# Differential attention in an encoder layer: the first map's row sums kept as a factor, each head's norm issued beside the next head, the first q projected during cross attention

## The chip, the cores and the metric

One core of a Trainium2 chip runs the whole kernel. The metric is the device time in microseconds (us) of one execution, of which the median over several runs is taken. All times below are in us unless marked ns.

## The reference, cut to what matters

The kernel computes one layer of an encoder with three branches (a state-space branch "S5", differential attention, and cross attention to a memory), merges the branches through gates, and adds a feed-forward part. Two sequences of 512 tokens, 1024 wide, are done together. Only the differential attention and the cross attention are touched here:

```python
def _rmsnorm(x, g):
    return x * rsqrt(mean(x * x, axis=-1) + EPS) * g          # EPS = 1e-6

def _diff_attention(q, k, v, lam, subln_g, lambda_init):      # 4 heads, 2 maps of width 64 each, values 128 wide
    s = einsum('bqhd,bkhd->bhqk', q, k) * 64 ** -0.5
    probs = softmax(s, axis=-1).reshape(..., 4, 2, Q_BLOCK, L)
    w = probs[:, :, 0] - lam * probs[:, :, 1]
    o = einsum('bhqk,bkhe->bqhe', w, v)
    return _rmsnorm(o, subln_g) * (1.0 - lambda_init)         # over the 128 values of a head

def _cross_attention(q, mk, mv):                              # 4 heads of width 128, 256 memory rows
    probs = softmax(einsum('blhd,bmhd->bhlm', q, mk) * 128 ** -0.5)
    return einsum('bhlm,bmhd->blhd', probs, mv)
```

Before attention, q and k of differential attention are rotated in their first 16 of 64 columns. Gates are columns of the same input projection; the kernel takes them through tanh and stores them until the merge.

## The kernel before, in words

**Number format.** Everything is float32. A product of matrices is made on TensorE in three passes: each operand is split into a high part (float32r) and a low part, and high times high, low times high and high times low are added up in one PSUM bank. `split` (lines 106 to 113) makes the parts: a copy on ScalarE for the high part (109), a subtraction on VectorE for the low part (110). `weight` (115) loads a block of weights, 128x1024, into `wf` and splits it into `wh` and `wl`. `mm3` (124) issues the three passes of one step (129, 130, 132), and `proj` (134) makes one projection of 128 output columns: for each of the two sequences a bank `bkmm`, 8 steps of three matmuls, 512 columns each. A projection is so 48 matmuls.

**Order of the work.** The kernel is written with the Tile framework. It has a scheduler that simulates a timeline (line 1265) and puts the instructions of each engine in an order of its own: an instruction that is traced later may be moved ahead, as far as data and buffers allow. Each engine then runs its own instructions strictly in that order and waits at each for what it needs from the others. `tc.issue_after(x)` (in `behind`, 302) keeps what is traced inside it from being put ahead of instruction x. Buffers are taken from pools in turn; in the stage of interest the eight PSUM banks are divided into mm=2 (projections), sc=3 (scores), tr=2 (transposes and small results) and oo=1 (the product with the values); line 413.

**Cross attention** (447 to 482). For each of four heads one projection makes q of both sequences, which is split. Then for each sequence four tiles of 128 queries: scores against 256 memory rows in three matmuls (463 to 465) into a bank `bksc`, `softmax_parts` (363: the negated row maximum on VectorE, 366; its scaling, 368; exp with the row sums on ScalarE, 371; the reciprocal of the sums, 373), the scaling of the exps by it (467), two transposes (470) into `bktr`, and their split into `xpTh` and `xpTl`. After the four tiles six matmuls with the values (476 to 478) into `bkoo`, a copy to `osb` (480) and a store (481). In the last head's loop the values of differential attention for its first two heads are projected (`v_half`, 426 to 445), and one gate.

**Differential attention** (593 to 618). For each head h: `qk_tile` (496) projects q for both sequences (both maps, 64 rows each), rotates it with a product and a shuffle on VectorE (503, 505), a product and a sum on POOL (506, 507), and scales it into a tile for each map (510, 511); then the same for k, where copies on ScalarE (514), subtractions on VectorE (516) and four small DMAs in each sequence (515, 517) lay out high and low parts. The two mm banks of a projection come free when 503 and 505 have read them. Gates, the second half of the values and, in head 3, parts of the merge (575) are traced between (lists `NG_D`, `NM`, `VPOS`, lines 38 to 40).

Then `attend(h, s, ...)` (520) for each sequence s. For each of four tiles of 128 queries: the scores of both maps (533, 534; two matmuls of 512 columns each), `softmax_parts` for each map, the second map's reciprocal times -lam (537), the first map's exps times its reciprocal (538), the combination e1 * r1 + e0 (539), four transposes (542), and a split into the quarter's half of `pH` and `pL`. After each two tiles, twelve matmuls of 256 columns with the values (546 to 548). When all four tiles are through, the norm over the head's 128 values: `oo` is copied to `osb` (550), transposed by four transposes (554), squared on ScalarE with the sums in `ss` (557), and `factor` (166) makes the root (Sqrt on ScalarE, 169), its reciprocal (170) and, by four transposes of the broadcast column (173), a bank `bc` that holds the factor in every row. One product (559) applies factor and weights to `osb`, which goes to DRAM (560); the merge reads it later.

ScalarE holds one table of functions at a time. Exp (371) and Sqrt (169) are in different ones, so each norm brings a table load before the Sqrt and one before the next Exp; the trace shows them as `ACT_TABLE_LOAD` at the line of the instruction that needs the table.

For the prediction, head and sequence of an `attend` are written as two digits, its tiles as 0 to 3 and its maps as a and b: "scores 3b" is the second map of the fourth tile, T(0) the four transposes of a tile 0, "0a" of the next half the first map of the tile after. "pH(1)" is the copy for tile 1.

Of the kernel before, what the change touches and what calls it, by code (L numbers as in the profile page):

```python
# [10 lines left out]
F32 = mybir.dt.float32  # L11
F32R = mybir.dt.float32r
I32 = mybir.dt.int32
AF = mybir.ActivationFunctionType
# [5 lines left out]
P = 128  # L20
L = 512
# [27 lines left out]
def encoder(ctx: ExitStack, tc: tile.TileContext, a, out):  # L49
# [113 lines left out]
            PE.matmul(ss[:, t : t + 1], acc[:, t * P : (t + 1) * P], onec[:, 0:1], start=(t == 0), stop=(t == nt - 1))  # L163
        return factor(ss, n, nt)

    def factor(ss, n, nt=4):

        rs = rp.tile([P, 4], F32, tag="rs", name="rs", bufs=4)
        S.activation(out=rs[:, :nt], in_=ss[:, :nt], func=AF.Sqrt, scale=1.0 / n, bias=epsc)
        V.reciprocal(rs[:, :nt], rs[:, :nt])  # L170
        bc = aux()
        for t in range(nt):
            PE.transpose(bc[:, t * P : (t + 1) * P], rs[:, t : t + 1].broadcast_to([P, P]), ident)
        return rs, bc
# [127 lines left out]
    def behind():  # L302

        return tc.issue_after(last_mm.ins)
# [55 lines left out]
        nc.sync.dma_start(bD[0, t], sg)  # L360
    phase.close()

    def softmax_parts(pool, col, sc, n, scale, nm):

        nb = col.tile([P, 1], F32, tag=nm + "nb", name="nb")
        V.tensor_reduce(out=nb, in_=sc, axis=AX.X, op=ALU.max, negate=True)
        if scale != 1.0:
            V.tensor_scalar_mul(nb, nb, scale)
        e = pool.tile([P, n], F32, tag=nm + "e", name="e")
        sm = col.tile([P, 1], F32, tag=nm + "s", name="sm")  # L370
        S.activation(out=e, in_=sc, func=AF.Exp, bias=nb, scale=scale, accum_out=sm)
        r = col.tile([P, 1], F32, tag=nm + "r", name="r")
        V.reciprocal(r, sm)
        return e, r
# [72 lines left out]
    for h in range(4):  # L447
# [6 lines left out]
        for s in range(NS):  # L454
            if 2 * h + s == VPOS[0]:
                vv = v_half(0)
            ms = slice(s * NMEM, (s + 1) * NMEM)
            pTh = slot("xT", [P, 2, L], F32R, "xpTh")
            pTl = slot("xT", [P, 2, L], F32R, "xpTl")
# [33 lines left out]

    LO, HI = slice(0, 64), slice(64, P)

    def qk_tile(mt, is_q):
        o = proj(a["w_in"][mt], xh, xl)
        m0, m1 = (slot("qk", [P, NT], F32R, n_) for n_ in ("m0", "m1"))
        kl = (None, None) if is_q else tuple(slot("qk", [P, NT], F32R, n_) for n_ in ("l0", "l1"))
        for s in range(NS):  # L500
# [16 lines left out]
                    nc.sync.dma_start(l_[other, cs].bitcast(F32), l_[own, cs].bitcast(F32))  # L517
        return (m0, m1) if is_q else (m0, m1, *kl)

    def attend(h, s, q, kk, v):  # L520
        cs = slice(s * L, (s + 1) * L)
        oo = bank("oo")
        vs = slice((h % 2) * P, (h % 2) * P + P)
        vh, vl = v
        for qh in range(2):
            pH = slot("pT", [P, 4, 2 * P], F32R, "pH")
            pL = slot("pT", [P, 4, 2 * P], F32R, "pL")
            for q2 in range(2):
                q0 = s * L + (2 * qh + q2) * P
                er = []  # L530
                for mp in range(2):
                    sc = bank("sc")
                    PE.matmul(sc, q[mp][:, q0 : q0 + P], kk[mp][:, cs], start=True, stop=False)  # L533
                    PE.matmul(sc, q[mp][:, q0 : q0 + P], kk[2 + mp][:, cs], start=False, stop=True)  # L534
                    er.append(softmax_parts(ap_, acol, sc, L, 1.0, f"d{mp}"))
                (e0, r0), (e1, r1) = er
                V.tensor_tensor(out=r1, in0=r1, in1=nlam, op=ALU.mult)
                V.tensor_scalar_mul(e0, e0, r0)
                V.scalar_tensor_tensor(out=e0, in0=e1, scalar=r1, in1=e0, op0=ALU.mult, op1=ALU.add)
                tr = aux()  # L540
                for j in range(4):
                    PE.transpose(tr[:, j * P : (j + 1) * P], e0[:, j * P : (j + 1) * P], ident)
                split(pH[:, :, q2 * P : (q2 + 1) * P], pL[:, :, q2 * P : (q2 + 1) * P], tr.rearrange("p (j q) -> p j q", j=4))
            od = oo[:, qh * 2 * P : (qh + 1) * 2 * P]
            for j in range(4):
                PE.matmul(od, vh[:, j, vs], pH[:, j, :], start=(j == 0), stop=False)
                PE.matmul(od, vh[:, j, vs], pL[:, j, :], start=False, stop=False)
                PE.matmul(od, vl[:, j, vs], pH[:, j, :], start=False, stop=(j == 3))
        osb = rp.tile([P, L], F32, tag="nsq", name="osb", bufs=2)
        S.copy(osb, oo)  # L550
        tr = aux()
        ss = rp.tile([P, 4], F32, tag="ss", name="ss", bufs=3)
        for t in range(4):
            PE.transpose(tr[:, t * P : (t + 1) * P], osb[:, t * P : (t + 1) * P], ident)
        sq = new_acc()
        for t in range(4):
            S.activation(out=sq[:, t * P : (t + 1) * P], in_=tr[:, t * P : (t + 1) * P], func=AF.Square, accum_out=ss[:, t : t + 1])
        _, bc = factor(ss, P)
        V.scalar_tensor_tensor(out=osb, in0=osb, scalar=g04, in1=bc, op0=ALU.mult, op1=ALU.mult)
        nc.sync.dma_start(bD[1, h, :, cs], osb)  # L560


    mg = [None] * KD
# [31 lines left out]
    for h in range(4):  # L595
        if h == 2:
            vv = v1 or v_half(1)
        q = qk_tile(4 + h, True)
        if h < 3:
            gates(NG_D[h][0])  # L600
        kk = qk_tile(8 + h, False)
# [13 lines left out]
        if h < 3:  # L615
            gates(NG_D[h][3])
        else:
            merge(0, b0, range(NM[2], KD), first=True)
    b2 = merge_in(2)
    merge(2, b2, range(KD))  # L620
    phase.close()
# [647 lines left out]
```

## Time and profile before

| what | value |
|---|---|
| median of 3 runs | 1674.23 us (1672.43 to 1677.33) |
| the profiled execution | 1674.95 us |
| its span, first to last instruction | 1673.2 us |
| mean granted clock of TensorE | 0.989 of full speed |
| bytes moved by DMA | 197.69 MB, 118 GB/s in the mean |
| first to last store of a norm's result (560) | 605.4 to 823.3 us of the span |
| first to last scores of cross attention start (463) | 422.4 to 523.4 us |

The profiled execution is one run of the kernel, recorded by the hardware. Its engines are PE (TensorE, matmuls), PEld (TensorE loading weights, which overlaps PE), DVE (VectorE), ACT (ScalarE), POOL (GpSimd) and SP (SyncE, whose queue issues the DMAs). An engine's busy share is the time in which it ran instructions; the idle time ahead of an instruction is put down to what ended it. A row of the view by stretches gives a window, then for each engine its busy time and, in brackets, its instructions, then the granted clock (1.00 is full speed), the mean busy share of the DMA engines and GB/s. A row of the timeline gives an instruction's start, its length, its engine, its line, out<-in and its shape, and in square brackets the time that its engine had been idle before it and what ended that. A row of the groups gives line, engine, operation, out<-in, count, then busy time and mean ns of one, then the idle time before the group's instructions and what ended it. Matmul records overlap: the next one starts before the record of the last one ends.

### The profile page before, as it was taken

The numbers are of one execution on the slowest core, as the hardware profiler recorded it, in microseconds if no ns is written. First come the engines' busy times: TensorE is split into PE (matmuls) and PEld (weight loads), VectorE is DVE, ScalarE is ACT, GpSimd is POOL, SyncE is SP. The second block draws the span as 40 slices with busy tenths as digits, with TensorE's granted clock in tenths as the row PEclk, the third lists the DMA queues.
The fourth block names the chain that finished last, engine by engine and source line by source line (L and its number), as shares of the span: only waits on it lengthen the run. The fifth ranks groups of instructions, "written<-read, shape, count | busy, mean of one in ns | idle before, by whom it ended". The sixth has DMA issues, their size and how long they took to land.

```text
span 1673.2 us, 21052 instructions
## 1 busy us (share of the span) xinstructions
PE 1625.6 (97%) x7916; PEld 1357.8 (81%) x7916; DVE 1076.2 (64%) x1788; ACT 622.1 (37%) x1092; POOL 391.7 (23%) x253
## 2 busy tenths in 40 slices
PE   5999999999999999999999999999999999999997
PEld 4788887888897788878888878888888888888887
DVE  7946898154554776777655668777777777743324
ACT  6534412245343456554323443223323223421121
POOL 0001000000001121120243346555554552500021
PEclk9999999999999999999999999999999999999999
DMA  9343252747111221333554432322222223741302
GB/s 367 114 154 127 96 170 89 222 174 241 46 57 64 88 57 40 112 107 120 182 187 127 140 101 79 125 87 82 83 86 79 88 79 115 252 133 52 84 17 101
DMA packets 79269, 197.69 MB, mean 118 GB/s; under 512 B 11072, under 2 KB 26688, under 8 KB 79168
## 3 DMA queue, kind: packets, MB, share of 16 engines
q1 hardware_dynamic: 79168, 196.35, 35.4%
q8 instruction: 62, 1.02, 0.3%
q14 instruction: 39, 0.32, 0.1%
HBM read 141.82 MB, written 50.30 MB: 115 GB/s over the span
## 4 chain that ended last, share of the span: by engine, by line
PE 79%; DVE 11%; DMA 3%; issue 2%; ACT 2%; POOL 1%; SPq 1%; DVEq 0%; POOLq 0%; ACTq 0%
PE bkmm L129 15%; PE bkmm L132 15%; PE bkmm L130 15%; PE bkmm L738 8%; PE bkmm L737 8%; PE bkmm L739 8%; DVE st L1140 1%; DVE wl L110 1%; PE bktr L1122 1%; POOL mg L587 1%; PE bksc L533 1%; DMA c_n<-cD 1%; PE bksc L534 1%; PE bkmm L438 1%; PE bkmm L439 1%
## 5 line engine op out<-in xcount | busy, mean ns | idle before, releaser
L109 ACT CAST wh<-wf 128x1024 fp32r<-128x1024 f32 (+4 forms) x164 | 142.3, 868 | 385.4 <-PE bkmm L130 225.9
L132 PE MATMUL bkmm<-xh,wl 128*128 128x512 f32 x640 | 252.1, 394 | 3.0 <-DVE wl L110 3.0
L129 PE MATMUL bkmm<-xh,wh 128*128 128x512 f32 x640 | 251.8, 393 | 2.3 <-DVE t L505 1.2
L130 PE MATMUL bkmm<-xl,wh 128*128 128x512 f32 x640 | 251.7, 393 | 0.0
L738 PE MATMUL bkmm<-tl,wh 128*128 128x512 f32 x612 | 240.1, 392 | 2.5 <-DVE tl L110 2.5
L737 PE MATMUL bkmm<-th,wh 128*128 128x512 f32 x612 | 239.9, 392 | 0.0
L739 PE MATMUL bkmm<-th,wl 128*128 128x512 f32 x612 | 238.5, 391 | 0.0
L110 DVE TENSOR_TENSOR wl<-wf,wh 128x1024 fp32r<-128x1024 f32 (+4 forms) x164 | 175.7, 1072 | 94.5 <-ACT wh L109 93.9
L129 PE MATMUL bkmm<-ah,wh 128*128 128x512 f32 (+1 forms) x408 | 147.1, 361 | 0.2 <-ACT wh L109 0.2
L130 PE MATMUL bkmm<-al,wh 128*128 128x512 f32 (+1 forms) x408 | 147.0, 360 | 0.0
L132 PEld LDWEIGHTS bkmm<-xh,wl 128*128 128x128 f32 x640 | 120.7, 189 | 29.1 <-DVE wl L110 3.8
L129 PEld LDWEIGHTS bkmm<-xh,wh 128*128 128x128 f32 x640 | 120.7, 189 | 28.7 <-DVE t L505 2.6
L130 PEld LDWEIGHTS bkmm<-xl,wh 128*128 128x128 f32 x640 | 120.5, 188 | 24.7 <-issue 0.4
L506 POOL TENSOR_TENSOR t<-t,rs 128x512 f32<-128x512 f32 x16 | 24.6, 1537 | 494.5 <-DVE t L505 494.5
L738 PEld LDWEIGHTS bkmm<-tl,wh 128*128 128x128 f32 x612 | 115.8, 189 | 28.1 <-DVE tl L110 4.2
L737 PEld LDWEIGHTS bkmm<-th,wh 128*128 128x128 f32 x612 | 115.8, 189 | 24.4 <-ACT th L109 0.3
L739 PEld LDWEIGHTS bkmm<-th,wl 128*128 128x128 f32 x612 | 115.5, 189 | 24.0
L132 PE MATMUL bkmm<-ah,wl 128*128 128x512 f32 (+1 forms) x408 | 127.4, 360 | 0.5 <-DVE wl L110 0.4
L802 POOL TENSOR_TENSOR up<-up,acc 128x512 f32<-128x512 f32 x44 | 85.1, 1957 | 149.4 <-DVE up L778 149.4
L862 DVE TENSOR_TENSOR y<-y,bkmm 128x512 f32<-128x512 f32 (+1 forms) x56 | 32.6, 608 | 111.4 <-PE bkmm L132 111.4
L153 POOL TENSOR_TENSOR acc<-acc,nsq 128x512 f32<-128x512 f32 (+1 forms) x32 | 38.0, 1187 | 241.2 <-ACT nsq L152 241.1
L132 PEld LDWEIGHTS bkmm<-ah,wl 128*128 128x128 f32 x408 | 76.9, 189 | 12.7 <-DVE wl L110 1.3
(585 smaller groups left out, 3272.3 us busy)
## 6 DMA issues: line engine op xcount, KB each, us to landing
wf<-in_w_in SPq DMA_DIRECT2D x40, 512.0 KB, 3.8
gD<-gt SPq DMA_DIRECT2D x24, 512.0 KB, 2.8
gl<-gD SPq DMA_DIRECT2D x24, 512.0 KB, 3.9
wf<-in_w_fg SPq DMA_DIRECT2D x22, 512.0 KB, 3.7
wf<-in_w_fu SPq DMA_DIRECT2D x22, 512.0 KB, 3.7
aD<-ac SPq DMA_DIRECT2D x22, 512.0 KB, 2.6
fl<-aD SPq DMA_DIRECT2D x22, 512.0 KB, 4.5
wf<-in_w_fo SPq DMA_DIRECT2D x16, 448.0 KB, 3.3
```

The costliest lines, as they stand in the source:

```text
L109: S.copy(hi, src)
L110: V.tensor_tensor(out=lo, in0=src, in1=hi.bitcast(F32), op=ALU.subtract)
L129: PE.matmul(outs[s], wh[:, ws], xh, start=(k == 0), stop=False)
L130: PE.matmul(outs[s], wh[:, ws], xl, start=False, stop=False)
L132: last_mm = PE.matmul(outs[s], wl[:, ws], xh, start=False, stop=(k == nk - 1))
L153: eng.tensor_tensor(out=acc[:, :n], in0=acc[:, :n], in1=sq[:, :n], op=ALU.add)
L506: PO.tensor_tensor(out=t2, in0=t2, in1=rope[1], op=ALU.mult)
L737: PE.matmul(ps, wh[:, ws_], th[:, o], start=(k == 0), stop=False)
L738: PE.matmul(ps, wh[:, ws_], tl[:, o], start=False, stop=False)
L739: PE.matmul(ps, wl[:, ws_], th[:, o], start=False, stop=(k == 3))
L802: PO.tensor_tensor(out=up, in0=up, in1=accs[s], op=ALU.mult)
L862: V.tensor_tensor(out=y[m][:, c : c + n], in0=y[m][:, c : c + n], in1=o_, op=ALU.add)
```

## The change

It has three parts, all between the last cross-attention head and the last differential head.

1. *The first map's row sums stay as a factor.* The map was e0/s0 - lam * e1/s1. Now it is e0 - lam * (s0/s1) * e1, which is s0 times as much for each query. For the first map `softmax_parts` takes a column of a 128x4 tile `s0` for its sums and leaves out the reciprocal; the scaling of the exps (538) goes; the small product (537) takes s0 as one more factor. The norm divides the factor out again: the mean of squares is s0 squared times as large, so the norm's epsilon must be multiplied by s0 squared. Two small operations on 128x4 make EPS * 128 * s0 * s0 and add it to the sums of squares, and the Sqrt has no bias of its own (`factor` gets an argument for it).
2. *The norm is issued beside the next head.* After the squares, `attend` no longer traces the factor, the product and the store, but puts them as a function into a list. The next `attend` calls it after its first half's value product, with `issue_after` that product's last matmul. The last norm is called after the head loop, behind the last projection matmul traced until then.
3. *The first q of differential attention is projected in cross attention.* Its `proj` is traced at the start of the last (head, sequence) pair of cross attention, and `qk_tile` of head 0 gets the two banks.

```diff
-    def factor(ss, n, nt=4):
+    def factor(ss, n, nt=4, bias=epsc):
...
-        S.activation(out=rs[:, :nt], in_=ss[:, :nt], func=AF.Sqrt, scale=1.0 / n, bias=epsc)
+        S.activation(out=rs[:, :nt], in_=ss[:, :nt], func=AF.Sqrt, scale=1.0 / n, bias=bias)
...
-    def softmax_parts(pool, col, sc, n, scale, nm):
+    def softmax_parts(pool, col, sc, n, scale, nm, sums=None):
...
-        sm = col.tile([P, 1], F32, tag=nm + "s", name="sm")
+        sm = col.tile([P, 1], F32, tag=nm + "s", name="sm") if sums is None else sums
         S.activation(out=e, in_=sc, func=AF.Exp, bias=nb, scale=scale, accum_out=sm)
+        if sums is not None:
+            return e, sm
         r = col.tile([P, 1], F32, tag=nm + "r", name="r")
         V.reciprocal(r, sm)
         return e, r
...
                 vv = v_half(0)
+            if 2 * h + s == 7:
+                q0 = proj(a["w_in"][4], xh, xl)
             ms = slice(s * NMEM, (s + 1) * NMEM)
...
-    def qk_tile(mt, is_q):
-        o = proj(a["w_in"][mt], xh, xl)
+    def qk_tile(mt, is_q, o=None):
+        o = o or proj(a["w_in"][mt], xh, xl)
...
+    norms = []
+
     def attend(h, s, q, kk, v):
...
+        s0 = acol.tile([P, 4], F32, tag="s0", name="s0", bufs=3)
         for qh in range(2):
...
             for q2 in range(2):
-                q0 = s * L + (2 * qh + q2) * P
+                qt = 2 * qh + q2
+                q0 = s * L + qt * P
...
-                    er.append(softmax_parts(ap_, acol, sc, L, 1.0, f"d{mp}"))
-                (e0, r0), (e1, r1) = er
-                V.tensor_tensor(out=r1, in0=r1, in1=nlam, op=ALU.mult)
-                V.tensor_scalar_mul(e0, e0, r0)
+                    er.append(softmax_parts(ap_, acol, sc, L, 1.0, f"d{mp}", None if mp else s0[:, qt : qt + 1]))
+                (e0, sm0), (e1, r1) = er
+                V.scalar_tensor_tensor(out=r1, in0=r1, scalar=nlam, in1=sm0, op0=ALU.mult, op1=ALU.mult)
                 V.scalar_tensor_tensor(out=e0, in0=e1, scalar=r1, in1=e0, op0=ALU.mult, op1=ALU.add)
...
-                PE.matmul(od, vl[:, j, vs], pH[:, j, :], start=False, stop=(j == 3))
+                pv = PE.matmul(od, vl[:, j, vs], pH[:, j, :], start=False, stop=(j == 3))
+            if qh == 0 and norms:
+                with tc.issue_after(pv.ins):
+                    norms.pop()()
...
-        _, bc = factor(ss, P)
-        V.scalar_tensor_tensor(out=osb, in0=osb, scalar=g04, in1=bc, op0=ALU.mult, op1=ALU.mult)
-        nc.sync.dma_start(bD[1, h, :, cs], osb)
+        V.scalar_tensor_tensor(out=s0, in0=s0, scalar=EPS * P, in1=s0, op0=ALU.mult, op1=ALU.mult)
+        V.tensor_tensor(out=ss, in0=ss, in1=s0, op=ALU.add)
+
+        def norm():
+            _, bc = factor(ss, P, bias=0.0)
+            V.scalar_tensor_tensor(out=osb, in0=osb, scalar=g04, in1=bc, op0=ALU.mult, op1=ALU.mult)
+            nc.sync.dma_start(bD[1, h, :, cs], osb)
+
+        norms.append(norm)
...
-        q = qk_tile(4 + h, True)
+        q = qk_tile(4 + h, True, None if h else q0)
...
             merge(0, b0, range(NM[2], KD), first=True)
+    with behind():
+        norms.pop()()
     b2 = merge_in(2)
```

## Prediction

> **What bounds the kernel now.** I read the page first: the share of each engine and the chain that ended last.
>
> ```profile
> span 1673.2 us, 21052 instructions
> PE 1625.6 (97%) x7916; PEld 1357.8 (81%) x7916; DVE 1076.2 (64%) x1788; ACT 622.1 (37%) x1092; POOL 391.7 (23%) x253
> PE 79%; DVE 11%; DMA 3%; issue 2%; ACT 2%; POOL 1%; SPq 1%; DVEq 0%; POOLq 0%; ACTq 0%
> ```
>
> TensorE (PE) is the bound. The change removes no matmul and no transpose (the built order of both kernels holds the same 7,679 TensorE rows; it differs only from the last cross-attention head to the last differential head), so it can only win or lose waits of PE. Next, busy time by stretches of 20 us. After the times come PE, PEld, DVE, ACT, POOL, the granted clock and DMA.
>
> ```profile
> 520.00:540.00 20.00, 18.12 (x84) 14.45 (x83) 7.68 (x22) 5.77 (x15) 2.59 (x2) 1.00 0.23 80
> 540.00:560.00 20.00, 17.93 (x76) 13.69 (x75) 10.38 (x17) 5.38 (x8) 8.60 (x6) 1.00 0.21 59
> 600.00:620.00 20.00, 18.98 (x125) 16.80 (x124) 16.26 (x33) 11.62 (x24) 5.39 (x4) 1.00 0.31 86
> 620.00:640.00 20.00, 19.76 (x156) 18.98 (x155) 11.80 (x28) 11.71 (x29) 0.00 (x0) 1.00 0.07 21
> 640.00:660.00 20.00, 17.70 (x105) 14.42 (x104) 14.83 (x38) 11.17 (x31) 0.00 (x0) 1.00 0.17 53
> 740.00:760.00 20.00, 16.56 (x77) 11.92 (x76) 19.45 (x35) 14.79 (x31) 4.26 (x2) 1.00 0.71 204
> ```
>
> PE idles in four places: the end of cross attention (1.88 + 2.07 us), the step from head 0 to 1 (1.02), head 1 (0.24 + 2.30) and the start of head 3 (3.44). Its steps, from timeline rows (start, length):
>
> ```profile
> 485.50 0.28 PE L438 MATMUL bkmm<-wh,xh 128*128 128x256 f32 x1
> 485.62 0.28 PE L463 MATMUL bksc<-mkvh,qh 128*128 128x256 f32 x1
> 524.89 0.60 PE L470 MATMUL bktr<-ident,e 128*128 128x128 f32 x4
> 525.24 0.48 PE L129 MATMUL bkmm<-xh,wh 128*128 128x512 f32 x1
> 525.56 0.39 PE L130 MATMUL bkmm<-xl,wh 128*128 128x512 f32 x1
> 525.79 0.39 PE L132 MATMUL bkmm<-xh,wl 128*128 128x512 f32 x1
> ```
>
> A matmul takes 0.12 us at 256 columns and 0.23 at 512, four transposes 0.35. A record lasts 0.39 but the next starts after 0.23, so each break loses 0.16 more than the idle column shows. With 5, 3, 6 and 6 breaks there, the places lose 4.75, 1.5, 3.5 and 4.4 us: 14.2 in all, the most that this change could win.
>
> Durations of the other engines, from the groups between 500 and 860 us (busy, mean ns):
>
> ```profile
> L366 DVE TENSOR_REDUCE nb<-bksc 128x1 f32<-128x512 f32 (+1 forms) x72 | 46.1, 652 | 19.1 <-PE bksc L534 11.8 <-PE bksc L465 7.1
> L110 DVE TENSOR_TENSOR pL<-bktr,pH 128x512 fp32r<-128x512 f32 x32 | 21.8, 681 | 1.7 <-ACT pH L109 1.7
> L538 DVE TENSOR_SCALAR e<-e,r 128x512 f32<-128x512 f32 x32 | 16.0, 503 | 0.6
> L373 DVE RECIPROCAL r<-sm 128x1 f32<-128x1 f32 x72 | 10.9, 156 | 13.8 <-ACT e L371 13.6
> L170 DVE RECIPROCAL rs<-rs 128x4 f32<-128x4 f32 x8 | 1.4, 178 | 10.2 <-ACT rs L169 10.2
> L110 DVE TENSOR_TENSOR xpTl<-bktr,xpTh 128x256 fp32r<-128x256 f32 x8 | 3.2, 417 | 6.4 <-ACT xpTh L109 6.4
> L467 DVE TENSOR_SCALAR e<-e,r 128x256 f32<-128x256 f32 x8 | 2.8, 350 | 0.2
> L371 ACT ACTIVATE e<-bksc,nb 128x512 f32<-128x512 f32 (+1 forms) x72 | 48.2, 670 | 24.4 <-DVE nb L366 21.4 <-DVE r L373 1.6 <-DVE nb L368 0.9
> L109 ACT CAST pH<-bktr 128x512 fp32r<-128x512 f32 x32 | 18.7, 585 | 29.6 <-PE bktr L542 29.3
> L109 ACT CAST vh<-bkmm 128x256 fp32r<-128x256 f32 x12 | 4.3, 380 | 4.5 <-PE bkmm L440 3.9 <-DVE vl L110 0.5
> L169 ACT ACT_TABLE_LOAD x8 | 10.3, 1283 | 0.1
> ```
>
> **The change, part by part.**
>
> *Row sums as a factor.* VectorE (DVE) loses 32 scalings (16.0 us) and 32 reciprocals (32 x 0.156 = 5.0). The 32 products with nlam stay one instruction. It gains 16 operations on 128x4; the trace has none of this kind, the nearest row is the reciprocal on 128x4 at 0.178, so 2.8 us (2.5 by the 128x1 reciprocal's 0.156, 10.4 if each took a full tile's 0.65). Net about -18 us of DVE, between -10.6 and -18.5. DVE is not the bound, and the chain from the second exp to the transposes (reciprocal, product, L539) keeps its length. So I count nothing by itself. In 740 to 760, where DVE is 97% busy, two scalings (1 us) would be felt; that is in the last place below. If DVE's slack elsewhere were gone, the same would count for each tile, in our favour.
>
> *Norms beside the next head.* Eight norms keep their work: four squares, a load of the Sqrt table, Sqrt, reciprocal, four transposes, a product, the store. The number of table loads stays 16 in the changed order, too. What moves: the Sqrt and the load back now stand in ScalarE's (ACT) queue among the exps of the next head, TensorE's broadcast transposes behind that head's first value product, the store behind the product in SP's queue. The loads and copies of weights that now stand behind the store are needed some 10 us later, so I count 0 for it, and up to 3 us if one came late. The win shows in the chain at 596 us:
>
> ```profile
> 597.67 1.28 ACT L169
> 599.28 1.28 ACT L371
> ```
>
> These two loads hold up ACT's copies of the next q and k, so that head 1's first scores wait for the k copies (the 1.5 us). In the new order the copies pass between the two loads, and I find only about 0.4 us: **-1.1**.
>
> Against it stands head 1. Score banks are three, and each is freed by its exp. The new order there is, on TensorE: norm transposes, T(0), 3 value matmuls, scores 3b, 13 value matmuls, T(1), scores of the next half 0a, then 0b. That is 0.35 + 0.35 + 0.36 + 0.46 + 1.56 + 0.35 + 0.46 = 3.9 us. Scores 0b need the bank of exp 3b. On ACT that exp stands behind: squares, pH, exp 2a, Sqrt load, Sqrt, load back. Their rows:
>
> ```profile
> 628.25 0.28 ACT L557 ACTIVATE acc<-bktr 128x128 f32<-128x128 f32 x1
> 629.26 0.71 ACT L371 ACTIVATE e<-bksc,nb 128x512 f32<-128x512 f32 x1
> 630.34 1.28 ACT L169 ACT_TABLE_LOAD   x1
> 631.63 0.30 ACT L169 ACTIVATE rs<-ss,epsc 128x4 f32<-128x4 f32 x1
> ```
>
> The four squares take 1.0 us and begin some 0.6 after the norm transposes. So 0.6 + 1.0 + 0.59 + 0.67 + 1.28 + 0.30 + 1.28 + 0.67 = 6.4: PE loses 2.5. After the scores (6.85) the value product needs pH(1), which follows two copies of 0.38 and its own 0.59: 7.75, another 0.9; scores 1a need the next exp, 8.4: another 0.5. One norm later the same: PE needs pH(1) 4.6 us after the norm transposes, ACT has it after 0.6 + 1.0 + 0.59 + 0.67 + 1.28 + 0.30 + 0.38 + 0.59 = 5.4; 0.8, 0.6 for the low half behind it (0.68) and 0.5 for the value bank behind the load back. Together 5.8 against 3.5 before: **+2.3**. The other five norms have 7 us or more of other matmuls between; I count 0 for them.
>
> The Trainium skill bears on this (ScalarE: Activation LUTs, "What ACT_TABLE_LOAD costs"): a switch of sets costs the 1283 ns load and a drain of about 1380 ns, 2.66 us in all. By it the two loads at the first norm would take 2.8 us more and the one load at the second 1.4, an estimate of 4.2 us on top of the sum. The load's length agrees; the drain doesn't show, since Sqrt starts 1.29 us after the load did (630.34 to 631.63), so I keep the trace.
>
> *First q in cross attention.* Before, the scheduler already ran this projection among the last block's scores and transposes (24 matmuls before, 24 between its transposes). Now all 48 stand ahead of that block's 12 scores, 8 transposes and 6 value matmuls, with nothing between; k's projection can't fill in, since both mm banks wait for q's rotation, which DVE does last.
>
> ```profile
> 486.18 0.42 DVE L366 TENSOR_REDUCE nb<-bksc 128x1 f32<-128x256 f32 x1 [1.09 <-PE bksc L465]
> 530.81 0.60 PE L470 MATMUL bktr<-ident,e 128*128 128x128 f32 x4
> 531.85 1.23 DVE L110 TENSOR_TENSOR wl<-wf,wh 128x1024 fp32r<-128x1024 f32 x1 [4.06 <-ACT wh L109]
> 533.66 0.68 DVE L503 TENSOR_TENSOR t<-bkmm,rc 128x512 f32<-128x512 f32 x1
> 535.05 0.50 PE L129 MATMUL bkmm<-xh,wh 128*128 128x512 f32 x1
> ```
>
> Before, from 530.81 to 535.05, PE did 4 transposes and 6 matmuls (1.7 us) in 4.24: 2.5 lost. Now DVE runs the whole block in a row: 4 reductions (0.42 at 256 columns), 8 small products and reciprocals (0.16 each, as the reciprocals' row), a wl (1.23), 4 scalings (0.35), 4 low halves (0.42) = 7.3, from 0.55 us on (three score matmuls and a record's tail); then, as before, 1.4 us from the rotation's start to PE's next matmul: 9.2. PE's own work in it is 1.4 + 0.7 + 1.4 = 3.5, so 5.7 are lost: **+3.2**. Ends: 2.5 lost (DVE's list hidden as before) and 8.5 (four pH-like copies of 0.38 and the exps' waits not overlapped). Line 109's wh for a gate stands ahead of the exps, so wl stands inside DVE's list. The three waits for rotations that follow stay as they are: 0.
>
> *Start of head 3.* DVE's list between k's last rotation and the first merge matmul is the same less two scalings; a pH waits behind a copy of k instead. 4.7 by the same walk against 4.4: **+0.3**, between -1 and +2.
>
> **Sum**: -1.1 + 2.3 + 3.2 + 0.3 = +4.7. The profiled execution took 1674.95 (span 1673.2), so 1679.7 in its own time; the median of the three runs is 0.7 lower. A walk holds only the waits that I found, so I round up: **1680 us**, 0.34% slower. A measurement tells about 0.3% (5 us) from no change.
>
> **The rivals.**
>
> *The waits hide in each other.* Head 1's loss comes later than cross attention's, and DVE's 18 us of relief could bring exps and transposes forward: half of the 4.7 stays. Also that the third edit does nothing, since that projection ran there already, belongs here. For it: PE is 97% busy and other work fills most gaps. 1676 us.
>
> *Not slower: the norms pay everywhere.* If ACT reaches exp 3b before TensorE wants its bank, that is, if TensorE comes there 6.4 us or more after the norm transposes instead of 3.9, the 1.5 + 3.5 + 4.4 us of the heads go and only +3.2 is paid: -6, 1668 us. For it: the chain at 597. Against it: the counted order of 0b.
>
> *Table pairs at two more norms.* In heads 2 and 3 the margin is only 1 to 2 us. Two more at the first norm's 3.9 us: 1688 us. This is in the range.
>
> *The clock.* Where PE idled longest in this trace, the clock fell (the column before the last two):
>
> ```profile
> 32.00:33.00 1.00, 0.00 (x0) 0.00 (x0) 1.00 (x2) 1.00 (x3) 0.00 (x0) 1.00 1.03 422
> 35.00:36.00 1.00, 1.00 (x2) 0.36 (x2) 1.00 (x5) 1.00 (x3) 0.00 (x0) 0.50 0.98 401
> 42.00:43.00 1.00, 1.00 (x4) 0.81 (x3) 0.90 (x8) 0.98 (x6) 0.00 (x0) 0.50 0.05 20
> ```
>
> The bare block is only 40% full. At half the clock for as long as here (35 to 43, 8 us), up to 4 us more: 1684. Against it: the longest single break that I count there is some 1.3 us, and the clock is 1.00 in all rows from 520 on. The Trainium skill (TensorE: Matmul & The Clock Gate, Part 1) lets the clock fall after an idle window of about 3.4 us; by that it doesn't fall here, and no run shows such a block yet.
>
> **How the numbers follow.** Slower (forecast 0.42, more norms or clock 0.10): 0.52. Waits hidden, within 0.3%: 0.33. Norms pay: 0.15. Range 1668 to 1688, from the second rival to the third. In these, the unknown ends (DVE's small operations, the bare block 2.5 to 7, head 3) lie inside.
>
> **What would show it.** Right: about 6 us lost in the last cross block, with a TensorE wait there for L467 and for the rotation; a wait of about 2.5 us of L533 on an exp behind the load back in head 1; no wait on the k copies at head 1's first scores; DVE about 18 us less busy. Wrong: PE full in head 1, or the cross block no barer than before; or the waits in places that I took for full.

## The result, and the profile after

The changed kernel takes 1680.38 us (median of 6 runs, 1679.04 to 1683.63) against 1673.93 (6 runs, 1672.43 to 1677.33): a ratio of 1.0041, 95% interval 1.0031 to 1.0052, so 0.41% slower. Its profiled execution took 1680.21, with a span of 1678.4.

In its lines, scores are 545 and 546, transposes of a tile 553, value products 557 to 559, norm transposes 568, squares 571, exp 372, the rotation 508 and 510, cross scores 468 to 470 and cross transposes 475. First the page of the changed kernel, span and engines:

```profile
span 1678.4 us, 20993 instructions
PE 1627.1 (97%) x7916; PEld 1360.1 (81%) x7916; DVE 1067.8 (64%) x1740; ACT 621.2 (37%) x1092; POOL 393.0 (23%) x253
```

The count of matmuls is the same, and VectorE lost 48 instructions (1788 to 1740) but only 8.4 us of busy time. Then the same six stretches as in the prediction, changed kernel (times; PE, PEld, DVE, ACT, POOL busy; granted clock; DMA):

```profile
520.00:540.00 20.00, 16.66 (x68) 12.65 (x67) 7.35 (x24) 5.92 (x16) 2.56 (x2) 0.83 0.16 57
540.00:560.00 20.00, 18.65 (x82) 15.07 (x81) 9.38 (x16) 5.51 (x9) 8.74 (x6) 0.99 0.22 62
600.00:620.00 20.00, 20.00 (x130) 18.08 (x130) 18.02 (x32) 12.07 (x22) 7.10 (x5) 1.00 0.42 115
620.00:640.00 20.00, 17.62 (x105) 15.21 (x104) 11.84 (x29) 11.55 (x32) 0.00 (x0) 0.83 0.00 1
640.00:660.00 20.00, 19.15 (x151) 18.20 (x150) 11.70 (x27) 13.93 (x35) 0.00 (x0) 1.00 0.12 41
740.00:760.00 20.00, 15.78 (x73) 10.65 (x71) 18.41 (x28) 13.59 (x23) 5.63 (x3) 1.00 0.62 170
```

Three things are to be seen. From 600 to 620 PE is full now. From 620 to 640 it isn't, and it was before. And in two stretches the granted clock is 0.83, where it was 1.00.

To find where the time went, the same TensorE instruction is taken from both timelines, at points up to which both have done the same work. Here the last matmul of a projection, first three times in the kernel before:

```profile
515.94 0.39 PE L132 MATMUL bkmm<-xh,wl 128*128 128x512 f32 x1
561.27 0.39 PE L132 MATMUL bkmm<-xh,wl 128*128 128x512 f32 x1
762.19 0.39 PE L132 MATMUL bkmm<-yh,wl 128*128 128x512 f32 x1
```

and then in the changed one:

```profile
515.07 0.39 PE L132 MATMUL bkmm<-xh,wl 128*128 128x512 f32 x1
563.63 0.39 PE L132 MATMUL bkmm<-xh,wl 128*128 128x512 f32 x1
768.06 0.39 PE L132 MATMUL bkmm<-yh,wl 128*128 128x512 f32 x1
```

The first is the end of the projection ahead of the first q's, the second that of the projection behind head 0's k, the third one of the merge behind the start of head 3. The difference goes from -0.87 to +2.36 and +5.87, and at 835 us, behind head 3, it is +6.30: **+3.2 us in the last cross block, +3.9 in the heads.** The rest of the 5.2 us between the spans lies ahead of the change (-0.87) and far behind it (-1.0). There the clock fell at other times in the two executions (in the kernel before for 3.4 us at 279 and 13.7 us at 996, in the changed one for 6.8 us at 1008), which the last section comes back to. The table holds such differences for all experiments, each for its profiled execution against that of the kernel before: the block between the marks at 516 and about 559 us, the heads from there to 835. They are of one execution each; the medians are of all runs.

| run | median us | ratio (95%) | cross block | heads |
|---|---|---|---|---|
| changed kernel | 1680.38 | 1.0041 (1.0031 to 1.0052) | +3.2 | +3.9 |
| p1_row_sums | 1671.66 | 0.9986 (0.9977 to 0.9995) | 0.0 | -1.9 |
| p2_norms | 1684.51 | 1.0061 (1.0048 to 1.0073) | 0.0 | +8.8 |
| p3_first_q | 1681.16 | 1.0042 (1.0030 to 1.0055) | +2.6 | +4.0 |
| p12_no_first_q | 1678.50 | 1.0025 (1.0014 to 1.0035) | 0.0 | +3.8 |
| f1_pads | 1685.15 | 1.0073 (1.0060 to 1.0085) | +3.2 | +5.5 |
| n1_newton_all | 1688.37 | 1.0087 (1.0073 to 1.0101) | +3.2 | -0.1 |
| n2_newton_p12 | 1686.61 | 1.0075 (1.0061 to 1.0088) | 0.0 | +1.9 |
| n3_newton_p1 | 1686.33 | 1.0075 (1.0062 to 1.0088) | 0.0 | -0.3 |
| n4_newton_all_same_layout | 1677.29 | 1.0014 (1.0005 to 1.0024) | +2.6 | +1.0 |
| g1_gate_in_head1_p12 | 1676.37 | 1.0016 (1.0007 to 1.0026) | 0.0 | +3.5 |
| g2_gate_in_head1_p1 | 1671.24 | 0.9985 (0.9977 to 0.9994) | 0.0 | -2.6 |
| r1_first_q_rotated_early | 1666.94 | 0.9963 (0.9949 to 0.9977) | -1.7 | -4.1 |

### The profile page after: what moved, and what is told of

It reads as the page before. It is cut to its first block, busy times and chain, and to the rows that moved or that the text cites. A ratio compares the mean times of both kernels' runs of the same rounds, so it can differ in the third digit from the quotient of the medians.

```text
span 1678.4 us, 20993 instructions
## 1 busy us (share of the span) xinstructions
PE 1627.1 (97%) x7916; PEld 1360.1 (81%) x7916; DVE 1067.8 (64%) x1740; ACT 621.2 (37%) x1092; POOL 393.0 (23%) x253
## 4 chain that ended last, share of the span: by engine, by line
PE 80%; DVE 10%; ACT 3%; DMA 2%; issue 2%; POOL 1%; SPq 1%; DVEq 0%; POOLq 0%; ACTq 0%
PE bkmm L129 15%; PE bkmm L132 15%; PE bkmm L130 15%; PE bkmm L760 8%; PE bkmm L761 8%; PE bkmm L759 8%; DVE st L1162 1%; DVE wl L110 1%; PE bktr L1144 1%; PE bkmm L441 1%; POOL mg L607 1%; PE bkmm L442 1%; PE bksc L545 1%; PE bkmm L443 1%; DMA c_n<-cD 1%
```

## The experiments

### The parts alone

Each of the three parts was put alone into the kernel before, and part 3 was taken out of the changed kernel; the diffs are those of the parts. (In p2_norms the norm keeps its bias, and the map its scaling.)

p1_row_sums: 

> The kernel before with part 1 alone (row sums kept as a factor, norm still inline). Theory (DVE is not the bound, its 18 us were slack): 1673 to 1675, no difference. Rival (the relief of DVE was felt in the heads, and the other parts hid that in the whole change): 1670 or less.

p2_norms: 

> The kernel before with part 2 alone (norms beside the next head, each with its reciprocals and scalings as before). TensorE's order in head 1 between the norm transposes and the first value product of that head is the changed kernel's. Theory (the two table loads stand ahead of the exp that frees a score bank): -1.9 us at the step from head 0 to 1, +3.6 in head 1 with the clock at half for 7 us, up to +2 at the start of head 3: 1676, between 1674.5 and 1678.5. Rival (the norms cost only together with part 1's order): 1672 to 1674.

p3_first_q: 

> The kernel before with part 3 alone (first q projected in cross attention). TensorE's order in the last cross block is the changed kernel's. Theory (the block is bare and PE waits there, as the changed kernel's trace showed): +3.2 us in that block, with the granted clock at half for about 7 us behind it; the heads keep the inline norms: 1677, between 1675.5 and 1679. Rival (what the block loses is won back behind it, since q is ready earlier): 1674, no difference.

p12_no_first_q: 

> The changed kernel with part 3 undone (q projected where it was). From head 1 on TensorE's order is the changed kernel's, row by row. Theory (places add up): the changed kernel's time less 3.2 us: 1677, between 1675.5 and 1678.5. Rival (one loss hides the other, so that taking the first away changes nothing): 1680.

**Part 3** costs what it cost in the whole change, in the same place: +2.6 in the cross block, and without it the block is back at 0.0 while the heads keep their loss (+3.8 against +3.9). So the two losses add up, and neither hides the other. By itself part 3 also changes the order in the heads (+4.0), so its median came out above what was expected.

**Part 1** is a gain, 0.14%, where nothing was expected. It comes almost wholly between 561 and 625 us (-1.7). The waits that the kernel before has at 609 to 612 us (0.44, 0.23 and 0.35 us) are not in that timeline, with the norms still inline. But the scheduler's order is another one too, from 567 us on, so whether VectorE's relief or the order made the gain no run tells.

**Part 2** alone loses 8.8 us in the heads, and its median, 1684.51, is far above what was expected. With part 1 the heads go from -1.9 to +3.8, so that there it costs 5.7. The sum of the parts (-3 + 10 + 7 us by the medians of that session) is far from the whole (+6): the scheduler makes an order of its own for each, and what part 2 alone loses beyond the whole change was not followed up.

### Is it the clock, or the waits? (f1_pads)

```diff
+    def pad(dst, n, after, w, x):
+        with tc.issue_after(after.ins):
+            for _ in range(n):
+                PE.matmul(dst, w, x, start=True, stop=True)
...
+                if lastx:
+                    pad(oo, NT_[lt], pv, mkh[h][:, 0:P], mvh[0][:, 0, :])
...
+                if (h, s, qt) == (1, 0, 1):
+                    pad(oo, 9, pv, vh[:, 0, vs], kk[0][:, 0:L])
```

> The changed kernel with 18 matmuls of 512 columns added whose results are overwritten: 9 among the transposes of the last cross block, 9 in head 1 ahead of the scores that wait for a bank. They add 4.1 us of work to TensorE, in places where it waited. Theory (half of each loss is the clock: the granted clock was 0.50 at 533 to 540 and 632 to 639 us of the changed kernel, and TensorE being busy there keeps it at 1.00): up to 2 us less in each place, less what the pads delay: 1678, between 1676 and 1680.5, and no row under 1.00 between 520 and 660. Rival (the loss is the waits alone): the same or slower, 1681 to 1685.

In all it was slower, as the rival had it, but not for its reason: the pads changed the scheduler's order in the heads (+5.5). The cross block can be read by itself. The stretches of f1_pads:

```profile
520.00:540.00 20.00, 17.96 (x84) 13.77 (x83) 7.35 (x24) 5.73 (x15) 1.64 (x2) 1.00 0.20 69
540.00:560.00 20.00, 17.65 (x75) 13.48 (x74) 10.34 (x16) 5.40 (x8) 8.84 (x7) 1.00 0.22 64
```

The clock stays at 1.00. PE did 9 pads (2.0 us) more in the block, and yet the block lost the same 3.2 us. And part 1 alone, which has the block of the kernel before, ended it at the same time (0.0) though in its profile the clock was 0.66 from 535 to 540 us. The other profiles say the same: eight kernels have the block of the kernel before; in five of them the clock was at half for 3.4 us there, in three it was not, and all eight took 45.3 to 45.4 us between the marks. So neither the clock nor PE's waits among the block's softmax set its end. Something else does, and the VectorE timeline shows it: the rotation of q and k. Line 503 (508, 522) reads each of the four banks. Kernel before, changed kernel and f1_pads:

```profile
533.66 0.68 DVE L503 TENSOR_TENSOR t<-bkmm,rc 128x512 f32<-128x512 f32 x1
539.93 0.69 DVE L503 TENSOR_TENSOR t<-bkmm,rc 128x512 f32<-128x512 f32 x1
546.28 0.69 DVE L503 TENSOR_TENSOR t<-bkmm,rc 128x512 f32<-128x512 f32 x1
553.41 0.69 DVE L503 TENSOR_TENSOR t<-bkmm,rc 128x512 f32<-128x512 f32 x1
```

```profile
535.66 0.68 DVE L508 TENSOR_TENSOR t<-bkmm,rc 128x512 f32<-128x512 f32 x1
555.53 0.69 DVE L508 TENSOR_TENSOR t<-bkmm,rc 128x512 f32<-128x512 f32 x1
```

```profile
536.81 0.68 DVE L522 TENSOR_TENSOR t<-bkmm,rc 128x512 f32<-128x512 f32 x1
556.59 0.69 DVE L522 TENSOR_TENSOR t<-bkmm,rc 128x512 f32<-128x512 f32 x1
```

The four rotations share one buffer pair and follow each other by 6.3 to 7.1 us, and from the first to the last it is 19.75, 19.87 and 19.78 us (19.2 in p3_first_q, whose block lost 2.6). PE's last wait ahead of the second mark is one for this chain, whatever PE does meanwhile: in the kernel before for k's parts, which are copied behind the third rotation, in the changed kernel for the bank that the fourth one frees.

```profile
554.34 0.47 PE L533 MATMUL bksc<-m,m 128*128 128x512 f32 x1 [0.92 <-DMA m<-m]
```

```profile
556.93 0.50 PE L129 MATMUL bkmm<-xh,wh 128*128 128x512 f32 x1 [1.35 <-DVE t L510]
```

What the change moved is the chain's start: 533.66 - 515.94 = 17.7 us behind the first mark before, 535.66 - 515.07 = 20.6 now, **2.9 us later**, since VectorE's list for the bare block stands ahead of it. The loss goes with the chain's end in every run with the bare block: in the changed kernel, f1 and n1 the last rotation starts 40.5 us behind the first mark in place of 37.5, and the block loses 3.2 to 3.3; in p3 and n4 it starts at 39.8, and the block loses 2.6.

### Are the table loads what head 1 loses? (Newton steps)

```diff
-            _, bc = factor(ss, P, bias=0.0)
+            _, bc = root(ss, None)
...
+        t_ = rp.tile([P, 4], F32, tag="rt", name="rt", bufs=2)
+        V.tensor_scalar(out=t_.bitcast(I32), in0=ss.bitcast(I32), scalar1=1, scalar2=None, op0=ALU.arith_shift_right)
+        V.tensor_scalar(out=rs.bitcast(I32), in0=t_.bitcast(I32), scalar1=-1.0, scalar2=float(0x5F3759DF), op0=ALU.mult, op1=ALU.add)
+        V.tensor_scalar_mul(ss, ss, -0.5)
+        for _ in range(3):
+            V.tensor_tensor(out=t_, in0=rs, in1=rs, op=ALU.mult)
+            V.tensor_tensor(out=t_, in0=t_, in1=ss, op=ALU.mult)
+            V.scalar_tensor_tensor(out=rs, in0=t_, scalar=1.5, in1=rs, op0=ALU.add, op1=ALU.mult)
```

(The factor sqrt(128) went into g04.) The same edit was made in the changed kernel (n1), without part 3 (n2), and with part 1 alone (n3).

n1_newton_all: 

> The changed kernel with the norms' root made on VectorE: an integer shift and subtraction for a first value and three Newton steps, 12 operations on 128x4 in place of Sqrt and reciprocal, so that no table is loaded in the heads. TensorE's order in head 1 up to the second first-half scores is the changed kernel's. Theory (table loads ahead of the exp are what head 1 loses): the 3.6 us of head 1 go: 1677, between 1675.5 and 1678. Rival (VectorE's longer chain, 12 x 0.16 = 1.9 us, or the banks take the place of the loads): 1680.

n2_newton_p12: 

> Parts 1 and 2 (no first q) with the root on VectorE as in the run with Newton steps. Theory: 1678.5 less 3.6 for head 1: 1675, between 1673.5 and 1676.5. Rival (nothing saved by the loads): 1678.5.

n3_newton_p1: 

> Part 1 alone (norm inline) with the root on VectorE. In part 1 alone the broadcast transposes of head 1 waited 2.6 us for the root. Theory (the loads held up the exps behind them): 1 to 3 us less than part 1 alone: 1669.5, between 1668 and 1671. Rival (the wait for the root stays, since VectorE's chain is as long as load, Sqrt and reciprocal, and nothing else was held up): 1671.7.

All three were slower than the kernels they came from, by 8 to 15 us. But the loss was not in the heads. It grew evenly from 880 to 1430 us, in the feed-forward part, which no edit touches. A stretch of n1_newton_all there:

```profile
1100.00:1200.00 100.00, 100.00 (x435) 81.22 (x434) 74.71 (x88) 29.05 (x37) 53.60 (x32) 1.00 0.23 81
```

PE is full at full clock, and does 435 matmuls in 100 us. The one thing that all three runs have, and that reaches so far, is the new buffer `rt`: two slots of 16 bytes, which push all that lies behind them in that part of SBUF by 32 bytes. So the next run gave the steps a buffer that was there already:

```diff
-        t_ = rp.tile([P, 4], F32, tag="rt", name="rt", bufs=2)
+        t_ = rp.tile([P, 4], F32, tag="rs", name="rt", bufs=4)
```

n4_newton_all_same_layout: 

> The run with Newton steps in all of the changed kernel, with one edit: the extra 128x4 buffer of the steps is taken from the pool tag of rs, so that no buffer behind it in SBUF moves by 32 bytes. The order of all engines is the same, row by row. In the first one each matmul behind 880 us took 0.2309 us where the kernel before took 0.2266, which added about 10 us by 1430. Theory (the place of the operands in SBUF slowed the matmuls): the pace goes back to 0.2266 and the time to 1678, between 1676.5 and 1679.5, 2 us under the changed kernel for head 1. Rival (the steps themselves slow something): 1688.

```profile
1100.00:1200.00 100.00, 100.00 (x443) 82.81 (x442) 77.12 (x89) 28.57 (x36) 55.37 (x34) 1.00 0.23 82
```

443 matmuls in the same stretch, 1677.29 us, as the theory had it. The order of all engines is the same in both runs, and from 880 to 1430 us n1 falls 10.3 us behind n4. So the place of the operands is what makes nearly all of the 11.1 us between them. And now the answer to the question, read in the heads, ahead of the slower part: without table loads they lose 1.0 us (n4), or nothing (n1), where they lose 3.9 with them, and 1.9 without part 3 (n2) where it was 3.8. **About 2 to 4 us of the heads' loss are the loads**, by the medians 3.1 (1680.38 - 1677.29); what the clock does because of their waits is in it. Nearly all of it lies in head 1: there (marks at 625 and 689 us) the changed kernel loses 3.6, n4 1.2 and n1 -0.3. n1 and n4 differ in the heads though their order is the same, and there the clock can be seen at work, 630 to 640 us in n1 and then in n4:

```profile
630.00:640.00 10.00, 8.70 (x63) 7.55 (x62) 8.29 (x32) 5.07 (x15) 0.00 (x0) 1.00 0.01 2
```

```profile
630.00:640.00 10.00, 8.69 (x50) 7.69 (x50) 6.90 (x22) 3.17 (x10) 0.00 (x0) 0.83 0.01 2
```

In n4 the clock was at half for 3.4 us from 633.4, in n1 not, and by 689 us n4 has lost 1.5 us against n1. So here, where PE has enough to do, the clock costs. To part 1 alone the Newton steps did harm, if anything: its heads kept -0.3 of the -1.9 us.

### Is it the exp behind the loads? (a gate moved)

```diff
-NG_D = ((0, 0, 1, 1), (0, 0, 0, 0), (0, 0, 1, 1))
+NG_D = ((0, 0, 1, 0), (0, 1, 0, 0), (0, 0, 1, 1))
```

g1_gate_in_head1_p12: 

> Parts 1 and 2 with one gate's projection traced in head 1 in place of head 0. Norms and table loads stay as they are, but on ScalarE the exp whose bank the scores 0b of the next half need now stands ahead of the squares and the loads. Theory (head 1 loses because that exp is behind the loads): no wait of the scores 0b, head 1's +3.6 falls to 1.5 or less: 1676.5, between 1675 and 1678. Rival (the loads are paid anyway, at the next exp): 1678.5.

The median fell as expected, but by the places not for that reason: the heads lose 3.5, as before (3.8), from 559 to 688 us 1.5 (1.7 with the gate in its old place), and the intervals of the two ratios overlap. First head 1 in the changed kernel, ACT and PE:

```profile
628.61 1.28 ACT L169 ACT_TABLE_LOAD   x1
629.90 0.20 ACT L169 ACTIVATE rs<-ss 128x4 f32<-128x4 f32 x1
630.13 1.28 ACT L372 ACT_TABLE_LOAD   x1
631.42 0.69 ACT L372 ACTIVATE e<-bksc,nb 128x512 f32<-128x512 f32 x1
632.25 0.71 PE L545 MATMUL bksc<-m,m 128*128 128x512 f32 x1 [2.28 <-ACT e L372]
```

Load, Sqrt, load, exp, and the scores that waited 2.28 us for that exp's bank. Then the same place with the gate moved:

```profile
627.20 1.28 ACT L169 ACT_TABLE_LOAD   x1
629.12 0.60 ACT L109 CAST pH<-bktr 128x512 fp32r<-128x512 f32 x1
629.74 1.28 ACT L372 ACT_TABLE_LOAD   x1
629.77 0.39 PE L555 MATMUL bkoo<-pH,vh 128*128 128x256 f32 x1 [1.33 <-ACT pH L109]
631.86 0.79 PE L543 MATMUL bksc<-m,m 128*128 128x512 f32 x1 [1.70 <-ACT e L372]
```

The scores 0b no longer wait, but the value product waits 1.33 for pH behind the first load, and the next scores 1.70 for the next exp behind the second. The rival was right here: the loads are paid anyway, at whatever comes next.

g2_gate_in_head1_p1: 

> Part 1 alone with the same gate moved. Between the norm transposes and the broadcast of the root in head 1 TensorE now has 36 value matmuls of 256 columns and two scores, 4.7 us, where part 1 alone had 10 and two scores and waited 2.6 us. Theory: that wait goes: 1669, between 1667.5 and 1670.5. Rival (the value matmuls are then missing at the end of head 1, where six scores follow each other with one exp each between): 1672 to 1675.

1671.24 against 1671.66: no difference that this tells. In part 1 alone the broadcast of the norm's root waited (first row of line 173):

```profile
630.37 0.62 PE L173 MATMUL bktr<-ident,rs 128*128 128x128 f32 x4 [2.61 <-DVE rs L170]
```

With the gate that wait is gone, but the heads gained only 0.7 (-2.6 against -1.9). New waits elsewhere took the rest, as the rival had it, though the largest up to the end of head 1 is at 602 us (1.21 us), not at the end of head 1.

### The chain of rotations, started earlier

If the chain of rotations sets the end of the cross block, part 3 did the wrong half: it moved the projection, and left the rotation behind the block's softmax. The last kernel takes part 1 and moves both.

```diff
-    open_tags(ves, v=4)
+    open_tags(ves, v=4, qf=2)
+    rq = ves.enter_context(tc.tile_pool(name="rq", bufs=1, reuse_waits="tile"))
...
+            if 2 * h + s == 7:
+                qf = qk_tile(4, True, "qf", rq)
...
-        q = qk_tile(4 + h, True)
+        q = qk_tile(4 + h, True) if h else qf
```

> Part 1 alone, and the first q not only projected but also rotated ahead of the last cross block, in buffers of its own (two tiles of q, 4 KB each, and two of 2 KB for the rotation, in SBUF for the whole stage). On VectorE both rotations of q now stand ahead of that block's softmax, so that the two banks come free and 32 matmuls of the next projections stand among the block's scores and transposes. Theory (in every kernel so far the first scores of head 0 ended the chain of four rotations, 6.3 us each, that starts behind the block's softmax; with two of them done earlier TensorE is the bound again): 3 to 5 us less than part 1 alone at that place, and the wait of 2.6 us in head 1 goes, because value matmuls stand there again: 1667, between 1665 and 1669. Rival (the k rotations are still behind the softmax and set the end as before): 1671.7. Rival (the buffers move others in SBUF and matmuls get slower, as in the first Newton run): over 1675.

**1666.94 us, ratio 0.9963 (0.9949 to 0.9977): faster than both kernels**, by 0.4% and 0.8%. Its rotations:

```profile
520.42 0.69 DVE L461 TENSOR_TENSOR t<-bkmm,rc 128x512 f32<-128x512 f32 x1 [3.17 <-PE bkmm L132]
527.22 0.69 DVE L461 TENSOR_TENSOR t<-bkmm,rc 128x512 f32<-128x512 f32 x1 [0.46 <-PE bkmm L132]
542.71 0.68 DVE L461 TENSOR_TENSOR t<-bkmm,rc 128x512 f32<-128x512 f32 x1
548.94 0.69 DVE L461 TENSOR_TENSOR t<-bkmm,rc 128x512 f32<-128x512 f32 x1
```

Counted from the first mark, here at 514.08, q's two start 11 us earlier than in the kernel before, as soon as its banks are full, where VectorE had been idle; k's come behind the softmax, 1.7 and 2.6 us earlier. No wait of PE for a rotation is left in the block. Its gain is 1.7, under the 3 to 5 expected. PE still waits there for the last block's softmax (1.01 and 0.88 us). And with the chain gone from PE's path the clock costs: in this execution it was at half for 3.4 us from 543.8, with PE busy all the time, which is 1.7 us of work. The heads gain another 2.2 against part 1 alone; there the broadcast of the root no longer waits, because 37 value matmuls stand between in place of 10. Together 3.9 of the 4.7 us between the medians. Behind 880 us the pace is the old one (443 matmuls from 1100 to 1200), so the new buffers did no harm there.

## Why the prediction was right, point by point

- **The sum.** +4.7 forecast for the profiled execution, 5.3 measured (1680.21 - 1674.95), 1680 against a median of 1680.38. That it came so close is luck in part. The places together are +7.1, not +4.7: the cross block as forecast, the heads 2.4 more. The 1.9 us that the profiled execution won back lie where the change touches nothing, and go with the clock.
- **PE is the bound, its work doesn't change.** So it was: 7916 matmuls in both, 1625.6 and 1627.1 us busy.
- **Row sums at nothing: the step that failed.** Alone they are worth 0.14% (0.05 to 0.23%), though VectorE is not the bound. And VectorE was relieved by 8.4 us, not 18, and below the lower bound given of 10.6: the product was taken for unchanged, and the 16 new operations for 2.8 us. Changed kernel, groups from 500 to 870 us:

```profile
L549 DVE SCALAR_TENSOR_TENSOR r<-r,nlam,s 128x1 f32<-128x1 f32 x32 | 9.6, 301 | 4.3 <-ACT e L372 3.8
L573 DVE TENSOR_TENSOR ss<-ss,s 128x4 f32<-128x4 f32 x8 | 3.7, 461 | 6.5 <-ACT acc L571 6.5
```

  The product that takes the sum as well costs 4.0 us more in 32, and the new operations 4.9 in all. The means of 301 and 461 ns are not what one of them takes, though: 28 of the 32 products take 0.20 to 0.22 us (0.15 to 0.16 before), and six of the eight additions 0.15 to 0.17, as the prediction had it. The other six records take 0.66 to 2.08 us each, together about 5 us more, which is half of what the relief fell short by. They wait for POOL, as the last section shows.
- **Norms: +1.5 in the heads (-1.1, +2.3, +0.3), measured +3.9.** By marks at 625, 689 and 762 us it is -1.9 at the step from head 0 to 1, +3.6 in head 1, +1.9 from there to 762 and +0.4 behind. The mechanism in head 1 is the one forecast: the wait for the exp behind the load back, 2.28 us against 2.5. But the exp was not the point: with it ahead of them the loads cost the same, at other waits. The gain at the step is not the deferral's alone, since part 1 without it has -1.7 there. The +1.9 at the start of head 3, forecast at +0.3 between -1 and +2, is not the loads: without any it is still 1.5 to 1.7 (n1, n2, n4). With part 1 alone it is -0.8, so it comes with the deferred norms; by which wait no run tells.
- **First q: +3.2, measured +3.2, by another way.** The walk added up PE's waits in the bare block, and held the three waits for rotations that follow for unchanged. They were not. Before, three of 0.5 to 0.9 us stand at the first scores and two projections; now there is one of 1.35. The block's end is set by the chain of rotations, which starts 2.9 us later. The number was near because VectorE's list, which the walk counted, is also what delays the chain; that PE's own waits would add up to it was wrong.
- **The clock** was a rival at some 0.1, and it did fall, in two places; at the first it cost nothing, for the reason just given. At the second it is part of head 1's +3.6; how much is open, since the 1.5 us between the two Newton runs stand for a fall of 3.4 us, the changed kernel's lasts 6.8, and no run has its own order at full clock. Rows of the changed kernel, one us each:

```profile
530.00:531.00 1.00, 0.62 (x3) 0.41 (x3) 1.00 (x5) 0.37 (x2) 0.00 (x0) 1.00 0.00 0
531.00:532.00 1.00, 0.41 (x2) 0.20 (x2) 1.00 (x7) 0.42 (x3) 0.00 (x0) 1.00 0.42 78
532.00:533.00 1.00, 0.41 (x2) 0.20 (x2) 0.78 (x5) 1.00 (x5) 0.00 (x0) 1.00 0.96 356
533.00:534.00 1.00, 0.57 (x2) 0.29 (x2) 0.96 (x4) 0.48 (x3) 0.00 (x0) 0.69 0.25 98
537.00:538.00 1.00, 1.00 (x4) 0.81 (x3) 0.00 (x0) 0.00 (x0) 0.87 (x1) 0.50 0.00 0
540.00:541.00 1.00, 1.00 (x6) 0.79 (x5) 0.53 (x1) 0.98 (x2) 0.00 (x0) 0.89 0.46 176
631.00:632.00 1.00, 0.00 (x0) 0.00 (x0) 0.00 (x0) 0.99 (x2) 0.00 (x0) 1.00 0.00 0
632.00:633.00 1.00, 0.75 (x2) 0.42 (x2) 0.67 (x3) 1.00 (x5) 0.00 (x0) 0.69 0.00 0
639.00:640.00 1.00, 1.00 (x8) 0.92 (x7) 0.53 (x2) 0.54 (x2) 0.00 (x0) 0.90 0.00 0
```

  It falls at 533.4 (0.69 is 0.38 us at full and 0.62 at half) after three us in which PE was 41 to 62% busy, and is back at 540.2, 6.8 us later; in head 1 from 632.4 to 639.2, again 6.8, after a single wait of 2.28 us. The prediction excluded it by the length of the longest break. It could have been seen in the trace before that this does not hold: there the clock fell at 279.3 us, behind a single wait of PE of 1.92 us. The Trainium skill (TensorE: Matmul & The Clock Gate, Part 1) says that the gate looks at a free-running window of 3413 ns, and lets the clock fall after at least one idle window. The 6.8 us are two such windows, and in each of the 14 traces all falls start on one grid of 3.413 us, so there the traces agree; but no window ahead of these two falls was idle all through, so a window need not be empty, and the measurement decides.
- **The load without a drain** held: Sqrt starts 1.29 us after its load in the changed kernel too (628.61 to 629.90), and the exp 1.29 us after the load back (630.13 to 631.42).

## What to carry to other kernels

A list of the bound engine's waits at a place tells that time is lost there, not what sets its end: look for the chain that delivers the next stage's first operand, and move its start, the whole of it, not only the matmuls at its head. A switch of function tables among dependent work was paid here wherever it stood; putting one instruction ahead of it only moved the wait. And a test kernel with a new buffer must keep the others where they were.

## What the hardware showed that was not expected

- **Where operands lie in SBUF changes the pace of matmuls.** 32 bytes more in one pool, nothing else: 443 matmuls in 100 us became 435 (0.2257 to 0.2299 us each), and 1677.29 us became 1688.37. Which operand has to lie where no run tells.
- **The clock falls on short waits, and not in every execution at the same place.** Near 280 us, where nothing was changed, PE waits once for 1.9 us in every kernel. In eleven of the 14 profiles, the kernel before among them, the clock fell there, and in three (the changed kernel, g1 and the last one) it did not. The grid of 3.413 us tells them apart: in the eleven the wait lies in one window, in which PE was busy for 0.43 to 0.44 of the time; in the three it is divided between two, of 0.82 to 0.94 and 0.50 to 0.61. The same holds all along: behind the first 10 us no window under 0.49 busy left the clock up, none over 0.68 brought it down, and between them both occur (busy by the matmul records, which overlap). Half the clock for 6.8 us is up to 3.4 us, of the size of the spread of single runs (1672.43 to 1677.33 for the kernel before).
- **A small VectorE operation with two inputs waits for POOL.** Each of the six long records of the product and the addition starts while POOL runs an instruction and ends 0.02 us behind it, so 0.2 us of work took up to 2.1. The four reciprocals there that start while POOL runs, with one input, take 0.15 to 0.18. One case in the changed kernel:

```profile
738.55 1.30 POOL L511 TENSOR_TENSOR t<-t,rs 128x512 f32<-128x512 f32 x1 [4.22 <-DVE t L510]
738.89 0.97 DVE L549 SCALAR_TENSOR_TENSOR r<-r,nlam,s 128x1 f32<-128x1 f32 x1
```
